# Layer norms as two fused VectorE operations a block, first norm without a trip through DRAM: one post-norm decoder layer on one core

## Chip, cores and metric

The kernel runs on one core of one Trainium2 chip. A core has TensorE (PE; its weight loads are listed as PEld), VectorE (DVE), ScalarE (ACT), GpSimd (POOL) and SyncE (SP, which here only issues transfers). The metric is the device time of one execution in microseconds (us), as a median over several runs.

## What is computed

One layer with 256 tokens of width 2048, all in float32. It has three sub-layers, and after each of them stands a layer norm over the residual sum:

```python
def layer_norm(x, g, b):
    mu = xf.mean(-1, keepdims=True)
    var = jnp.square(xf - mu).mean(-1, keepdims=True)
    return (xf - mu) * lax.rsqrt(var + LN_EPS) * g + b

y = hybrid_mixer(x, ...)              # two attention branches, gates, w_out
x = layer_norm(ALPHA * x + y, ln_g[0], ln_b[0])
y = mem_cross_attention(x, mem, ...)  # 4 heads into 256 memory tokens
x = layer_norm(ALPHA * x + y, ln_g[1], ln_b[1])
y = swiglu(x, w_ffn_in, w_ffn_out)    # width 5632
x = layer_norm(ALPHA * x + y, ln_g[2], ln_b[2])
```

## The kernel before, in words

**Products.** The 256 tokens are two tiles of 128 (`tt`). Every float32 operand is split into a rounded part and what the rounding leaves, and a product is three matmuls (L221 to L223). Weights stream from DRAM in chunks of 256 rows by 512 columns (`chunk_in`, L193): SP loads a chunk into `raw` (5 buffers), ScalarE writes the rounded half (L116), VectorE subtracts (L117), both into `hl` (4 buffers) or, for chunks that stay on chip, into a `b8` tile. A chunk serves 12 matmuls of 512 columns, 6 for each tile. Where `product` is called with `seq=8` (L242 to L253), the last eight chunks are used for the first tile alone, stay on chip, and then serve the second tile; there each third of four chunks (`i % 4 == 2`) has its subtraction done by GpSimd. Two products have `seq=8`: the first of the feed-forward (L827) and the last of the kernel (L848).

**Activations** are needed transposed, with their features on the partitions, as `Quad`s of 512 features by 256 tokens. `to_quad` (L153) makes half of one from a block of 128 tokens by 512 columns: four 128x128 transposes on TensorE (L156) into a PSUM tile `aux`, then a split (ScalarE L116, VectorE L117). `turn` (L168) makes a whole one from DRAM: four loads (L176), four 32x32-block transposes on VectorE (L181), a ScalarE copy (L182) and a VectorE subtraction (L184).

**Layer norms.** The class `Norm` (L664) adds a product to the residual on VectorE (L680) and takes its statistics (L681). `scales` (L683) aggregates them (L685), has GpSimd compute rstd with two tiny operations (L149, L150), and VectorE -mean * rstd (L689). `block` (L692) normalises 512 columns in place: ScalarE t * rstd - mean * rstd (L695), VectorE times g (L696), then plus b (L698), on GpSimd in the first norm and on even blocks of the second, on VectorE on its odd blocks. `run` (L700) does this block by block and makes the quads `lag` blocks later; blocks of columns named in `far` are written to DRAM (`keep`, L190) and come back through `turn`. `finish` (L722) is the last norm: ScalarE (L735), but VectorE for block 0 (L733), then VectorE times g (L739), GpSimd or VectorE plus b (L741), and the output (L742).

**Order.** The norms' steps are a generator in the queue `side`; `product` takes `steps` of it after each chunk, so that they are emitted between the chunks. The order in which the program emits is the priority from which a scheduler, at compile time, lays down each engine's fixed queue. The first norm (L772, both tiles, `lag` 6, quads 2 and 3 through DRAM) is emitted between chunks of the memory keys' product (`kc`, L774); its quads feed the query product `qc` (L779). The second norm (L811) runs tile by tile: the norm of tile 0 beside the `w_o_mem` products of tile 1, that of tile 1 beside the first tile's half of the first feed-forward product (L827). The last norm's `finish` is called as soon as a tile of the last product is done (L843).

Of the kernel before, what the change touches and what calls it, by code (L numbers as in the profile page):

```python
# [10 lines left out]
F32 = mybir.dt.float32  # L11
F32R = mybir.dt.float32r
AF = mybir.ActivationFunctionType
ALU = mybir.AluOpType
AX = mybir.AxisListType

P = 128
S = 256
NT = S // P
# [18 lines left out]
KC = 2  # L38
NTURN = 2
W = 512  # L40


class Side:
    """Work that is emitted in small steps between the chunks of the main products."""

# [20 lines left out]
def trunk(ctx: ExitStack, tc: tile.TileContext, a, out: bass.AP):  # L66
    nc = tc.nc
# [3 lines left out]
    work = ctx.enter_context(tc.tile_pool(name="work", bufs=2))  # L71
# [3 lines left out]
    side = Side()  # L75
    last = [None]
    later = []
# [9 lines left out]
    def nm(s):  # L87
        count[0] += 1
        return f"{s}_{count[0]}"
# [16 lines left out]
    class Quad:  # L106
        """Four blocks [128, 256] and what their rounding leaves, as operands of products."""

# [9 lines left out]

    # ---- constants
    ident = const.tile([P, P], F32, name="ident")  # L120
# [6 lines left out]
    for tt in range(NT):  # L127
        k = P * (tt + 1)
# [18 lines left out]
    def rstd(dst, var, scale):  # L147
        """(var * scale + eps) ** -0.5"""
        nc.gpsimd.tensor_scalar(dst, var, scale, EPS, op0=ALU.mult, op1=ALU.add)  # L149
        nc.gpsimd.tensor_tensor(dst, dst, mhalf, op=ALU.pow)  # L150

    # ---- transposes of [128 tokens, 512] into a quad
    def to_quad(q, tt, src):  # L153
# [10 lines left out]

    # ---- the same for 256 tokens, from DRAM: the loads put columns 128 a .. 128 a + 127 into partitions
    # 32 a .. 32 a + 31, so that transposes of 32 by 32 are all that is left. Partition p of block k holds
    # column 4 p + k (mixed), or column 32 k + p % 32 of those (not mixed).
    def turn(q, src, mixed=True):  # L168
# [22 lines left out]

    # ---- products with streamed weights: [256 tokens, kts * 128] @ [kts * 128, n]
    def chunk_in(pieces, c, n, held=False, mixed=False, fine=None, eng=None):  # L193
# [31 lines left out]
    def product(act, pieces, steps=1, before=None, first=None, seq=0, stream_seq=0, done=None):  # L225
        """act: quads; pieces: DRAM views of the weights' columns. The last seq chunks of weights stay on
        chip, and the first 128 tokens go through them before the others do."""
        n = sum(w.shape[1] for w in pieces)
        kts = pieces[0].shape[0] // P
        nchunk = kts // KC  # L230
        out = [ps_acc() for _ in range(NT)]
        for c in range(nchunk - seq):
            w = chunk_in(pieces, c, n, mixed=act[c * KC // 4].mixed, fine=first if c == 0 else None)
            if first is not None and c == 0:
                for _ in first:
                    pass
            if before is not None:
                before(c)
            for tt in range(NT):
                chunk_mm(out[tt], act, tt, c, kts, n, w)  # L240
            flush()
            side.step(steps)  # L242
        if seq:
            ws = []
            for i, c in enumerate(range(nchunk - seq, nchunk)):
                ws.append(chunk_in(pieces, c, n, held=i >= stream_seq, mixed=act[c * KC // 4].mixed, eng=nc.gpsimd if i % 4 == 2 else None))
                chunk_mm(out[0], act, 0, c, kts, n, ws[-1])
                side.step(steps)
            done(0, out[0])
            for i, c in enumerate(range(nchunk - seq, nchunk)):  # L250
                chunk_mm(out[1], act, 1, c, kts, n, ws[i])
                side.step(steps)
            done(1, out[1])  # L253
        elif done is not None:
            for tt in range(NT):
                done(tt, out[tt])
        return out
# [5 lines left out]

    # ---- inputs
    x, mem = a["x"][0], a["mem"][0]
# [19 lines left out]

    # ---- the weights of the latents
    ukT, uv = [], []
# [26 lines left out]

    # ---- indexer queries: [hi; lo] of a head on the partitions
    qi = []
# [18 lines left out]

    # ---- indexer keys, latents
    kvg = row_of(a["kv_norm_g"][0], LAT, "kvg")
# [9 lines left out]
    for tt in range(NT):  # L347
        sl = slice(tt * P, (tt + 1) * P)
        p = ps[tt]
# [31 lines left out]

    # ---- keys and values of the heads from the latents
    khT, vh = [], []
# [47 lines left out]

    # ---- attention of four heads
    def attention(q, kT, v, bias, slopes, oT, causal):
# [147 lines left out]

    # ---- gate of the first branch, before its sigmoid
    ma = [b8(F32) for _ in range(NT)]
# [5 lines left out]

    # ---- block attention: one block, so causal over all keys  # L590
    oTb = [None, None]
# [12 lines left out]
    for g in range(2):  # L604
# [4 lines left out]
        if g == 0:  # L609
            pass  # L610
    # the first branch must be done
    while oTa[1] is None or any(gen.__name__ == "dsa" for gen in side.queue):
# [34 lines left out]

    # ---- residual and layer norm
    tok = []
# [14 lines left out]
    class Norm:  # L664
        """Residual sums and the layer norm over them."""

# [15 lines left out]

        def scales(self, tt):  # L683
            mv = work.tile([P, 2], F32, tag="lnmv", name=nm("lnmv"))
            nc.vector.bn_aggr(mv, self.stats[tt])  # L685
            r = work.tile([P, 1], F32, tag="lnr", name=nm("lnr"))
            rstd(r, mv[:, 1:2], 1.0)
            m = work.tile([P, 1], F32, tag="lnm", name=nm("lnm"))
            nc.vector.tensor_scalar(m, mv[:, 0:1], r, -1.0, op0=ALU.mult, op1=ALU.mult)  # L689
            return r, m  # L690

        def block(self, tt, j, sc):  # L692
            cs = slice(j * W, (j + 1) * W)
            t = tok[tt][:, cs]
            nc.scalar.activation(t, t, AF.Identity, bias=sc[1], scale=sc[0])  # L695
            nc.vector.tensor_tensor(t, t, self.rows[0][:, cs], op=ALU.mult)  # L696
            eng = nc.vector if self.i > 0 and j % 2 else nc.gpsimd
            eng.tensor_tensor(t, t, self.rows[1][:, cs], op=ALU.add)  # L698

        def run(self, tts, lag, far=()):  # L700
            """Blocks of 512 columns: norm, then transposes some steps later; those in far through DRAM."""
            if self.quads is None:
                self.quads = [Quad() for _ in range(4)]
            sc = {tt: self.scales(tt) for tt in tts}
            todo = [(tt, j) for j in range(4) for tt in tts]
            spills = {j: spill() for j in far}
            for i in range(len(todo) + lag):
                if i < len(todo):
                    tt, j = todo[i]
                    self.block(tt, j, sc[tt])  # L710
                    if j in far:
                        keep(spills[j], tt, tok[tt][:, j * W:(j + 1) * W])
                if i >= lag:
                    tt, j = todo[i - lag]
                    if j not in far:
                        to_quad(self.quads[j], tt, tok[tt][:, j * W:(j + 1) * W])
                    elif tt == tts[-1]:
                        for _ in turn(self.quads[j], spills[j]):
                            yield
                yield  # L720

        def finish(self, tt):  # L722
            mv = work.tile([P, 2], F32, tag="lnmv", name=nm("lnmv"))
            nc.vector.bn_aggr(mv, self.stats[tt])
            r = work.tile([P, 1], F32, tag="lnr", name=nm("lnr"))
            rstd(r, mv[:, 1:2], 1.0)
            m = work.tile([P, 1], F32, tag="lnm", name=nm("lnm"))
            nc.vector.tensor_scalar(m, mv[:, 0:1], r, -1.0, op0=ALU.mult, op1=ALU.mult)
            for j in range(4):
                cs = slice(j * W, (j + 1) * W)  # L730
                t = tok[tt][:, cs]
                if j == 0:
                    nc.vector.tensor_scalar(t, t, mv[:, 0:1], r, op0=ALU.subtract, op1=ALU.mult)  # L733
                else:
                    nc.scalar.activation(t, t, AF.Identity, bias=m, scale=r)  # L735
            for j in range(4):
                cs = slice(j * W, (j + 1) * W)
                t = tok[tt][:, cs]
                nc.vector.tensor_tensor(t, t, self.rows[0][:, cs], op=ALU.mult)  # L739
                eng = nc.vector if j % 2 else nc.gpsimd  # L740
                eng.tensor_tensor(t, t, self.rows[1][:, cs], op=ALU.add)  # L741
                nc.sync.dma_start(out[0, tt * P:(tt + 1) * P, cs], t)  # L742

# [25 lines left out]

    # ---- cross-attention  # L770
    w_kv = a["w_kv_mem"][0]
    side.add(n1.run(range(NT), 6, (2, 3)))  # L772
    side.step(2)
# [40 lines left out]

    # ---- feed-forward
    hT = []
# [56 lines left out]
```

## Time and profile before

| what | us |
|---|---|
| median of 3 runs | 1504.6 |
| lowest and highest run | 1503.08, 1506.91 |
| profiled execution, first to last instruction | 1506.3 |

For the profiled execution no time is listed beside its span. Busy shares are of the span. In a timeline a row is: start, length, engine, line, operation, output<-inputs, shapes, how many instructions it merges, and in brackets how long the engine had been idle and what ended that. A matmul's length there contains its pipeline; the next one starts sooner. Groups by line give: how many, busy us, mean ns, and idle time before. `PEclk` is the share of TensorE's full clock that was granted.

### The profile page before, as it was taken

To read this page: it belongs to the slowest core of one execution; us is meant where nothing else is said; L and a number is where in the kernel's file an instruction comes from. 1 tells how busy PE (TensorE), PEld (TensorE's weight loads), DVE (VectorE), ACT (ScalarE), POOL (GpSimd) and SP (SyncE) were. 2 spreads that over 40 slices of the span, in tenths; PEclk is the share of its full clock that TensorE was granted. 3 is DMA by queue.
4 is the path that set the end of the run, shared out by engine and by line. 5 is a ranking of instruction groups with operands and counts; after the bars stand their busy time and mean duration, and the time that the engine had idled before them with its cause. 6 is when DMAs were issued, how large, how long until landed. Compare 5 with 4: busy or idle time off the path is not lost.

```text
span 1506.3 us, 17772 instructions
## 1 busy us (share of the span) xinstructions
PE 1464.6 (97%) x6640; PEld 1214.9 (81%) x6640; DVE 929.2 (62%) x1145; ACT 684.2 (45%) x798; POOL 55.6 (4%) x63
## 2 busy tenths in 40 slices
PE   7999999999999999889989999999999999999996
PEld 5988888888888887677878888888888888888885
DVE  6666986575756665776784555555455455545455
ACT  4645456454444443354753444444344444333342
POOL 0010000000000000040030000000000000000003
PEclk9999999999999999899999999999999999999998
DMA  9966667777667789749636667776777777666662
GB/s 272 235 181 185 193 207 233 220 251 224 206 200 224 230 257 281 192 141 298 204 117 201 208 210 222 222 220 204 231 217 204 223 219 248 193 200 190 194 218 88
DMA packets 201623, 318.71 MB, mean 212 GB/s; under 512 B 18880, under 2 KB 60992, under 8 KB 201536
## 3 DMA queue, kind: packets, MB, share of 16 engines
q1 hardware_dynamic: 201536, 317.57, 69.7%
q8 instruction: 52, 0.85, 0.2%
q14 instruction: 35, 0.29, 0.1%
HBM read 299.70 MB, written 17.83 MB: 211 GB/s over the span
## 4 chain that ended last, share of the span: by engine, by line
PE 51%; DVE 3%; DMA 1%; ACT 1%; issue 1%; POOL 0%; SPq 0%; ACTq 0%; DVEq 0%
PE acc L222 17%; PE acc L223 17%; PE acc L221 17%; DVE b L696 1%; DMA raw<-in_w_kv_mem 1%; DVE b L739 1%; PE aux L156 0%; ACT b L116 0%; DVE b L117 0%; DVE b L698 0%; DVE b L741 0%; DVE hl L117 0%; DVE lnst L681 0%; DVE b L680 0%; PE aux L261 0%
## 5 line engine op out<-in xcount | busy, mean ns | idle before, releaser
L117 DVE TENSOR_TENSOR hl<-raw,hl 128x1024 fp32r<-128x1024 f32 (+2 forms) x493 | 595.8, 1217 | 414.2 <-ACT hl L116 413.0
L116 ACT ACTIVATE hl<-raw 128x1024 fp32r<-128x1024 f32 (+2 forms) x495 | 516.2, 1051 | 592.4 <-PE acc L223 537.3
L222 PE MATMUL acc<-hl,b 128*128 128x512 f32 (+1 forms) x1976 | 771.8, 391 | 13.7 <-DVE hl L117 13.7
L221 PE MATMUL acc<-hl,b 128*128 128x512 f32 (+1 forms) x1976 | 769.5, 391 | 2.4 <-ACT b L182 1.7
L223 PE MATMUL acc<-hl,b 128*128 128x512 f32 (+1 forms) x1976 | 769.7, 390 | 1.1 <-DVE b L184 0.9
L222 PEld LDWEIGHTS acc<-hl,b 128*128 128x128 f32 x1976 | 373.3, 189 | 91.6 <-DVE hl L117 16.6
L221 PEld LDWEIGHTS acc<-hl,b 128*128 128x128 f32 x1976 | 373.3, 189 | 79.2 <-ACT b L182 2.5
L223 PEld LDWEIGHTS acc<-hl,b 128*128 128x128 f32 x1976 | 373.2, 189 | 78.8 <-DVE b L184 2.4
L181 DVE STREAM_TRANSPOSE tr<-turn 128x256 f32<-128x256 f32 (+1 forms) x156 | 71.3, 515 | 105.7 <-DMA turn<-spill 84.5
L182 ACT ACTIVATE b<-tr 128x1024 fp32r<-128x1024 f32 (+1 forms) x39 | 39.5, 1016 | 123.0 <-DVE tr L181 119.6
L184 DVE TENSOR_TENSOR b<-tr,b 128x1024 fp32r<-128x1024 f32 (+1 forms) x39 | 45.3, 1167 | 3.6 <-ACT b L182 3.0
L116 ACT ACTIVATE b<-aux 128x512 fp32r<-128x512 f32 (+1 forms) x44 | 23.2, 538 | 29.3 <-PE aux L262 15.5
L117 DVE TENSOR_TENSOR b<-aux,b 128x512 fp32r<-128x512 f32 (+1 forms) x44 | 26.1, 610 | 11.9 <-ACT b L116 11.7
L117 POOL TENSOR_TENSOR hl<-raw,hl 128x1024 fp32r<-128x1024 f32 x2 | 5.6, 2802 | 718.7 <-ACT hl L116 718.7
L222 PE MATMUL acc<-b,b 128*128 128x512 f32 x72 | 28.0, 391 | 0.3 <-DVE b L117 0.3
L221 PE MATMUL acc<-b,b 128*128 128x512 f32 x72 | 28.0, 393 | 0.1
L223 PE MATMUL acc<-b,b 128*128 128x512 f32 x72 | 27.9, 389 | 0.0
L117 DVE TENSOR_TENSOR b<-raw,b 128x1024 fp32r<-128x1024 f32 x16 | 23.1, 1461 | 7.7 <-ACT b L116 7.7
L261 PE MATMUL aux<-b,b 128*128 128x256 f32 (+1 forms) x80 | 21.9, 282 | 0.0
L116 ACT ACTIVATE b<-raw 128x1024 fp32r<-128x1024 f32 x18 | 18.4, 1059 | 5.9 <-DMA raw<-in_w_ffn_out 5.4
L262 PE MATMUL aux<-b,b 128*128 128x256 f32 (+1 forms) x80 | 21.0, 279 | 0.0
L260 PE MATMUL aux<-b,b 128*128 128x256 f32 (+1 forms) x80 | 20.8, 274 | 0.0
(129 smaller groups left out, 531.8 us busy)
## 6 DMA issues: line engine op xcount, KB each, us to landing
raw<-in_w_ffn_in SPq DMA_DIRECT2D x176, 512.0 KB, 4.5
raw<-in_w_in SPq DMA_DIRECT2D x143, 512.0 KB, 4.2
raw<-in_w_ffn_out SPq DMA_DIRECT2D x88, 512.0 KB, 4.2
raw<-in_w_out SPq DMA_DIRECT2D x32, 512.0 KB, 5.6
spill<-stage SPq DMA_DIRECT2D x56, 256.0 KB, 4.1
turn<-spill SPq DMA_DIRECT2D x112, 128.0 KB, 3.1
raw<-in_w_o_dsa SPq DMA_DIRECT2D x16, 512.0 KB, 4.5
raw<-in_w_o_moba SPq DMA_DIRECT2D x16, 512.0 KB, 4.2
```

The lines of the kernel that those rows point to most:

```text
L116: nc.scalar.activation(hi, src, AF.Copy)
L117: (eng or nc.vector).tensor_tensor(lo, src, f(hi), op=ALU.subtract)
L181: nc.vector.transpose(tr[:, i, :], v[:, i])
L182: nc.scalar.activation(hi, tr, AF.Copy)
L184: nc.vector.tensor_tensor(lo, tr, f(hi), op=ALU.subtract)
L221: nc.tensor.matmul(o[:, :n], xh, hi[:, kk, :n], start=k == 0, stop=False)
L222: nc.tensor.matmul(o[:, :n], xh, lo[:, kk, :n], start=False, stop=False)
L223: nc.tensor.matmul(o[:, :n], xl, hi[:, kk, :n], start=False, stop=k == kts - 1)
L260: nc.tensor.matmul(o, lh, rh, start=start, stop=False)
L261: nc.tensor.matmul(o, lh, rl, start=False, stop=False)
L262: nc.tensor.matmul(o, ll, rh, start=False, stop=stop)
L696: nc.vector.tensor_tensor(t, t, self.rows[0][:, cs], op=ALU.mult)
```

## The change

A block is now centred and scaled by two VectorE operations, `(t - mean) * g` and then `* rstd + b`. ScalarE and GpSimd no longer touch the blocks (GpSimd still computes rstd), and -mean * rstd is gone. The first norm runs with `lag` 4 and no `far` blocks: all its quads are made by `to_quad`. `finish` uses the same two operations, with the centring of two blocks ahead of the first scaling, and each block's output after its scaling. And the subtraction of each third of four held chunks goes from GpSimd to VectorE. Removed comments and docstrings are left out here.

```diff
@@ product, chunks with seq
-                ws.append(chunk_in(pieces, c, n, held=i >= stream_seq, mixed=act[c * KC // 4].mixed, eng=nc.gpsimd if i % 4 == 2 else None))
+                ws.append(chunk_in(pieces, c, n, held=i >= stream_seq, mixed=act[c * KC // 4].mixed))
@@ class Norm
         def scales(self, tt):
             mv = work.tile([P, 2], F32, tag="lnmv", name=nm("lnmv"))
             nc.vector.bn_aggr(mv, self.stats[tt])
             r = work.tile([P, 1], F32, tag="lnr", name=nm("lnr"))
             rstd(r, mv[:, 1:2], 1.0)
-            m = work.tile([P, 1], F32, tag="lnm", name=nm("lnm"))
-            nc.vector.tensor_scalar(m, mv[:, 0:1], r, -1.0, op0=ALU.mult, op1=ALU.mult)
-            return r, m
-
-        def block(self, tt, j, sc):
+            return mv[:, 0:1], r
+
+        def center(self, tt, j, sc):
             cs = slice(j * W, (j + 1) * W)
             t = tok[tt][:, cs]
-            nc.scalar.activation(t, t, AF.Identity, bias=sc[1], scale=sc[0])
-            nc.vector.tensor_tensor(t, t, self.rows[0][:, cs], op=ALU.mult)
-            eng = nc.vector if self.i > 0 and j % 2 else nc.gpsimd
-            eng.tensor_tensor(t, t, self.rows[1][:, cs], op=ALU.add)
+            nc.vector.scalar_tensor_tensor(t, t, sc[0], self.rows[0][:, cs], op0=ALU.subtract, op1=ALU.mult)
+
+        def scale(self, tt, j, sc):
+            cs = slice(j * W, (j + 1) * W)
+            t = tok[tt][:, cs]
+            nc.vector.scalar_tensor_tensor(t, t, sc[1], self.rows[1][:, cs], op0=ALU.mult, op1=ALU.add)
+
+        def block(self, tt, j, sc):
+            self.center(tt, j, sc)
+            self.scale(tt, j, sc)
...
         def finish(self, tt):
-            mv = work.tile([P, 2], F32, tag="lnmv", name=nm("lnmv"))
-            nc.vector.bn_aggr(mv, self.stats[tt])
-            r = work.tile([P, 1], F32, tag="lnr", name=nm("lnr"))
-            rstd(r, mv[:, 1:2], 1.0)
-            m = work.tile([P, 1], F32, tag="lnm", name=nm("lnm"))
-            nc.vector.tensor_scalar(m, mv[:, 0:1], r, -1.0, op0=ALU.mult, op1=ALU.mult)
+            sc = self.scales(tt)
+            for j in range(2):
+                self.center(tt, j, sc)
             for j in range(4):
+                self.scale(tt, j, sc)
+                if j + 2 < 4:
+                    self.center(tt, j + 2, sc)
                 cs = slice(j * W, (j + 1) * W)
-                t = tok[tt][:, cs]
-                if j == 0:
-                    nc.vector.tensor_scalar(t, t, mv[:, 0:1], r, op0=ALU.subtract, op1=ALU.mult)
-                else:
-                    nc.scalar.activation(t, t, AF.Identity, bias=m, scale=r)
-            for j in range(4):
-                cs = slice(j * W, (j + 1) * W)
-                t = tok[tt][:, cs]
-                nc.vector.tensor_tensor(t, t, self.rows[0][:, cs], op=ALU.mult)
-                eng = nc.vector if j % 2 else nc.gpsimd
-                eng.tensor_tensor(t, t, self.rows[1][:, cs], op=ALU.add)
-                nc.sync.dma_start(out[0, tt * P:(tt + 1) * P, cs], t)
+                nc.sync.dma_start(out[0, tt * P:(tt + 1) * P, cs], tok[tt][:, cs])
@@ cross-attention
-    side.add(n1.run(range(NT), 6, (2, 3)))
+    side.add(n1.run(range(NT), 4))
```

## Rows read from the trace of the kernel before

**Rows 1.** The page: each engine's busy us, share of the span and instructions.

```profile
PE 1464.6 (97%) x6640; PEld 1214.9 (81%) x6640; DVE 929.2 (62%) x1145; ACT 684.2 (45%) x798; POOL 55.6 (4%) x63
```

**Rows 2.** Busy time by stretch: us, PE, PEld, DVE, ACT, POOL, PEclk, DMA share, GB/s.

```profile
660.00:680.00 20.00, 15.82 (x65) 12.26 (x65) 19.70 (x15) 12.01 (x17) 14.08 (x8) 0.83 0.33 97
680.00:700.00 20.00, 20.00 (x88) 16.26 (x88) 13.89 (x18) 8.98 (x10) 0.00 (x0) 1.00 1.09 280
...
760.00:780.00 20.00, 17.12 (x76) 13.41 (x74) 19.58 (x23) 14.49 (x20) 8.77 (x7) 0.91 0.38 123
```

**Rows 3.** Timeline of VectorE, then of GpSimd, at the first norm.

```profile
656.70 0.38 DVE L685 BATCH_NORM_AGGREGATE lnmv<-lnst 128x2 f32<-128x24 f32 x2
657.48 1.23 DVE L117 TENSOR_TENSOR hl<-raw,hl 128x1024 fp32r<-128x1024 f32 x1 [0.40 <-ACT hl L116]
...
660.27 11.56 DVE L696 TENSOR_TENSOR b<-b,b 128x512 f32<-128x512 f32 x8 [0.36 <-ACT b L695]
671.75 5.63 DVE L117 TENSOR_TENSOR hl<-raw,hl 128x1024 fp32r<-128x1024 f32 x3
...
657.58 2.07 POOL L150 TENSOR_TENSOR lnr<-lnr,mhalf 128x1 f32<-128x1 f32 x2
661.09 14.08 POOL L698 TENSOR_TENSOR b<-b,b 128x512 f32<-128x512 f32 x8 [1.44 <-issue]
```

**Rows 4.** Timeline of TensorE behind the first norm: two waits.

```profile
674.09 0.80 PE L222 MATMUL acc<-hl,b 128*128 128x512 f32 x1 [3.77 <-DVE hl L117]
...
707.69 0.50 PE L222 MATMUL acc<-hl,b 128*128 128x512 f32 x1 [0.91 <-DVE hl L117]
```

**Rows 5.** Groups of instructions by line and shape, 640 to 800 us: GpSimd's additions.

```profile
L698 POOL TENSOR_TENSOR b<-b,b 128x512 f32<-128x512 f32 x12 | 20.3, 1717 | 7.3 <-DVE b L696 5.9 <-issue 1.4
```

**Rows 6.** The fused operation with a scalar per partition elsewhere: VectorE's groups, 130 to 180 us.

```profile
L561 DVE SCALAR_TENSOR_TENSOR score<-stage,widx,score 128x256 f32<-128x256 f32 x15 | 7.3, 483 | 0.6
L561 DVE SCALAR_TENSOR_TENSOR score<-stage,widx,score 128x128 f32<-128x128 f32 x15 | 5.2, 347 | 0.4
```

**Rows 7.** Timeline at the second norm: VectorE, ScalarE, then TensorE.

```profile
763.34 1.76 DVE L698 TENSOR_TENSOR b<-b,b 128x512 f32<-128x512 f32 x1
765.02 0.67 DVE L680 SCALAR_TENSOR_TENSOR b<-b,acc 128x512 f32<-128x512 f32 x1
765.62 0.68 DVE L698 TENSOR_TENSOR b<-b,b 128x512 f32<-128x512 f32 x1
...
773.43 3.18 DVE L117 TENSOR_TENSOR b<-raw,b 128x1024 fp32r<-128x1024 f32 x1 [0.17 <-ACT b L116]
...
768.56 4.84 ACT L116 ACTIVATE b<-raw 128x1024 fp32r<-128x1024 f32 x5
...
761.71 0.66 PE L156 MATMUL aux<-ident,b 128*128 128x128 f32 x4
...
768.16 0.39 PE L221 MATMUL acc<-hl,b 128*128 128x512 f32 x1
...
779.01 0.66 PE L156 MATMUL aux<-ident,b 128*128 128x128 f32 x4 [0.47 <-POOL b L698]
...
785.29 0.40 PE L223 MATMUL acc<-hl,b 128*128 128x512 f32 x1
```

**Rows 8.** Timeline of the end: first tile's sum, second tile's last matmul and norm.

```profile
1484.48 0.69 DVE L680 SCALAR_TENSOR_TENSOR b<-b,acc 128x512 f32<-128x512 f32 x1 [6.84 <-PE acc L223]
...
1491.98 0.39 PE L223 MATMUL acc<-b,b 128*128 128x512 f32 x1
...
1493.78 0.68 DVE L680 SCALAR_TENSOR_TENSOR b<-b,acc 128x512 f32<-128x512 f32 x1
...
1495.22 0.26 DVE L724 BATCH_NORM_AGGREGATE lnmv<-lnst 128x2 f32<-128x24 f32 x1
...
1495.85 0.55 POOL L150 TENSOR_TENSOR lnr<-lnr,mhalf 128x1 f32<-128x1 f32 x1
...
1502.40 0.69 DVE L741 TENSOR_TENSOR b<-b,b 128x512 f32<-128x512 f32 x1
```

## The prediction

> **What bounds the kernel now.** I read the page first: TensorE is busy 1464.6 us of a span of 1506.3 [rows 1]. Only its 41.7 us of idle time and what it runs at a lowered clock can be won, whatever VectorE (62%) or ScalarE (45%) save. The stretches show where: most are like 680 to 700, full and at full clock, 88 matmuls in 20 us, so 0.227 us each and 2.72 us for a chunk's twelve; 660 to 680 and 760 to 780 have TensorE at 15.82 and 17.12 us and clock 0.83 and 0.91, with VectorE full (19.70, 19.58) [rows 2]. These are the first and second norm. The third place is the end, where after the last matmul nothing but the last norm is left [rows 8].
>
> Then the timelines. **First norm:** VectorE takes 11.56 us for eight multiplications by g, and only then the three weight splits, for the first of which TensorE waits 3.77 us, until 674.09 [rows 3, 4]. GpSimd's additions run beside this, eight in 14.08 us. The reader is to see that the two engines slow each other: in the second norm a VectorE addition took 1.76 us beside GpSimd and 0.68 right afterwards, and a split 3.18 us against 1.23 [rows 7, 3]. **Second norm:** from 761.71 to 768.16 and from 779.01 to 785.29 TensorE does transposes and a few matmuls in fits [rows 7]. These are 12.7 us; 28 transposes at 0.66 us for four would be 4.6 us even at that pace, and eight matmuls 1.8, so some 6 to 7 us are lost. **End:** the last matmul is over at 1492.4, but the residual sum starts at 1493.78, because VectorE is still in the first tile's norm; the last write of the norm ends at 1503.09 [rows 8].
>
> A measurement of this kernel can tell about 0.3%, 4.5 us, from no change.
>
> **Price of the new operation.** The fused operation with two SBUF tensors and a scalar per partition took 483 ns for 256 columns and 347 for 128 [rows 6], so 136 ns per 128 columns and 483 + 2 x 136 = 755 ns for 512. The next independent one starts about 0.07 us before the end of the one in front (765.02 + 0.67 against 765.62 [rows 7]): one each 0.69 us. Where a scaling follows its own centring I count the whole 0.755. A block is then 1.445 us, and eight are 11.6 us: just what the eight multiplications take now beside GpSimd [rows 3]. VectorE gains nothing in length; what it gains is that ScalarE's and GpSimd's steps (1.7 us an addition [rows 5]) no longer stand before and behind it.
>
> **The end.** The aggregation starts at 1495.22 and ends at 1495.48. A centring needs only the mean, so two can run while GpSimd makes rstd: to 1496.94. Six operations are left from 1496.88: 5 x 0.69 + 0.755 = 4.2, to 1501.1 against 1503.09, 2.0 us less. But GpSimd may not get at its operands meanwhile. In the first norm its two power operations took 2.07 us next to VectorE's L117, while one alone took 0.55 [rows 3, 8]: 1.0 us more. That L117 also reads two SBUF tensors, as a centring does; no row shows the fused form beside GpSimd. If the first centring goes in front of rstd and the second in between, rstd ends 1.45 us later than its 1496.40, the first scaling starts at 1497.85, the last ends at 1502.05: 1.0 us less. I take this end, since the two-tensor L117 is the nearest row. The first tile's norm also ends earlier by as much, and the residual sum starts 1.0 us earlier (at most 1.4, when TensorE is done). Sum 2.0 us, at most 3.4.
>
> The Trainium skill, "SBUF — State Buffer", section "Who interferes with whom", says that a VectorE instruction with two SBUF inputs and a GpSimd instruction that reads SBUF exclude each other for a whole instruction. It names no exception for the fused form, so by it the end gains 2.0 us; with no such exclusion it would gain 3.4. The pair of power operations agrees with it for the plain two-tensor form.
>
> **The first norm.** The first centring can start at 657.1, as the aggregations end; the first multiplication now starts at 660.27 [rows 3]. With 11.6 us and up to 1.7 us for rstd, the sixteen end between 668.8 and 670.5, against 671.83. The split behind them takes 1.2 us instead of a third of 5.63, so that TensorE could go on at 670.0 to 671.7 instead of 674.09: 2.4 to 4.1 us. Against this stand the quads that now go through TensorE: four more `to_quad`, 16 transposes (at most 2.6 us, inside the wait if one is left), and four more splits. All eight such splits are emitted ahead of the later weight chunks and each costs VectorE about 0.6 us, as a plain operation of this size (0.68 less 0.07 [rows 7]): if all go first, that is 4.8 us more and TensorE goes on at 674.8 to 676.5, up to 2.4 us later. If one more weight chunk slips behind them, a further 1.6 us or so are lost. From -4 to +4 us; nothing decides the queue's order, and I take the middle, 0.
>
> **The trip through DRAM.** It takes away four writes, eight loads on SP's queue, eight VectorE transposes and two splits. While these run, TensorE is full (20.00 of 20 us [rows 2]), so the trip itself is hidden; its place in the queue may have made the one wait at 707.69, 0.91 us [rows 4]. I take 0.4 of 0 to 0.9.
>
> **The second norm.** VectorE gets more to do: 16 fused operations (8 blocks x 1.445 = 11.6) for 12 plain ones (12 x 0.6 = 7.2), and two weight splits of 1.2 that GpSimd had, one before the norm; it loses four tiny operations and what GpSimd's additions and splits added to it: 1.1 on an addition and 2.0 on a split in the rows shown [rows 7], with two or three more such places. So 6.8 more against 5 to 6 less: about even. What changes is the path: rstd, then ScalarE, VectorE, GpSimd is now rstd, then one VectorE operation; and the second tile's norm no longer queues on ScalarE behind five weight conversions of 4.84 us together [rows 7]. I count 2.4 of the 7 us lost there as won: between nothing, if VectorE's length decides, and 6. If weight splits slip behind the norm here as well, 4 us are lost instead.
>
> **GpSimd's split in the last product** costs nothing: VectorE waits 6.84 us for TensorE before the first tile's sum [rows 8], and 2 x 1.2 us fit. Without that cover it would be 2.4 us.
>
> **Sum:** 2.0 + 0 + 0.4 + 2.4 = 4.8 us. The profiled execution's 1506.3 (1.7 over the median) becomes 1501.5, the median 1504.6 becomes **1499.8**.
>
> **Rivals.** *VectorE's length decides (25%).* Both norms stay as long as they are, since one VectorE operation replaces work that three engines shared; only the end is won. For it: VectorE is full in both stretches [rows 2] and 11.6 equals 11.56. Against it: the 3 us of later start. 1504.6 - 2.0 = 1502.6, no change that can be told.
>
> *The norms stop holding TensorE (18%).* The splits fall between the fused operations, so TensorE hardly waits: 3.4 at the end, 3 in the first norm, 0.9, and 5 in the second: 12 us, 1492. For it: every mutual slowdown goes. Against: the count of VectorE's work just made.
>
> *Weight splits queue behind the norm (12%), slower.* The place is VectorE's queue in both norms. Four `hl` buffers hold 48 matmuls, 10.9 us at 0.227 (half as long where a chunk serves only one tile): it decides when the norm work put in one piece in front of a split is longer than that. Sixteen fused operations and eight splits would be 11.6 + 4.8 = 16.4 us. Price: 4 us in the first norm, 4 in the second, 2 more at the lowered clock around a long wait (a granted clock of 0.83 over 20 us [rows 2] is 3.4 us of work at full clock, part of it inside the wait), less 2.0 at the end: 8 us, 1512.6.
>
> *The change does less than it says (5%):* the trip through DRAM was hidden and nothing else moves: that ends as the first rival does.
>
> **Numbers.** The forecast has 40%, with a range of its own of 1497.5 to 1502.5 (0 to 0.9 for the trip, two us either way in a norm). Three fifths of it lie below 1500.1, the bound of faster: 0.24; with the second rival 0.18, and 0.05 from the first and the last, if the end gains all of 3.4 and a norm a little: 0.47. Slower 0.12, and one hundredth for an order that I have not thought of: 0.13. The rest, 0.40, is no change. The range runs from the second rival's 1492 to 1508, which takes in a slower rival at half its price and leaves out about one in ten on either side.
>
> **What would show it.** Right: the residual sum of the second tile at 1492.8 or earlier by this clock, the last write some 1.0 us sooner after it; fused operations of about 0.755 us, never over 1; GpSimd with only tiny operations; wait before the first norm's weight split between 2 and 5 us; less than 6 us lost in the second. Wrong: fused operations that differ much from 0.755 us, a wait of TensorE for a weight split of over 6 us in either norm, more than one stretch at a lowered clock in each, or any change in the feed-forward between the second norm and the end.

## The result, and the profile after

| | before | after |
|---|---|---|
| median, us (4 runs each) | 1505.76 | 1489.49 |
| lowest and highest, us | 1503.08, 1506.97 | 1485.75, 1490.49 |
| profiled execution's span, us | 1506.3 | 1483.6 |

The changed kernel takes 0.9892 of the time before, with a 95% interval of 0.9876 to 0.9908: 16.3 us faster, where 4.8 were forecast. The measured time lies outside the range given.

The page of the changed kernel, its line of engines, answers to [rows 1]:

```profile
PE 1455.7 (98%) x6656; PEld 1209.4 (82%) x6656; DVE 919.0 (62%) x1151; ACT 669.6 (45%) x778; POOL 21.1 (1%) x43
```

TensorE is busy 8.9 us less although it has 16 transposes more, and its idle time falls from 41.7 to 27.9 us. GpSimd drops from 55.6 to 21.1.

**Where the time went.** The two profiles can't be compared from their start: at the last pair of residual sums ahead of the first norm (VectorE, L680) they already differ by 7.6 us (653.19 against 645.55), although the instructions up to there stand in the same order in both kernels. That scatter belongs to no part of the change (the same changed kernel, run again as e8_after below, comes to this point at 650.39), so the stages are counted from those sums on. The boundaries are instructions that both kernels have: the second copy of the memory keys' product (ScalarE L425), the first residual sum of the `w_o_mem` product (L680), the end of the last matmul, the end of the span. The first three in the kernel before, then in the changed one:

```profile
653.19 1.28 DVE L680 SCALAR_TENSOR_TENSOR b<-b,acc 128x512 f32<-128x512 f32 x2
684.58 0.60 ACT L425 ACTIVATE stage<-acc 128x512 f32<-128x512 f32 x1 [0.76 <-PE acc L223]
749.72 1.28 DVE L680 SCALAR_TENSOR_TENSOR b<-b,acc 128x512 f32<-128x512 f32 x2
...
645.55 1.28 DVE L680 SCALAR_TENSOR_TENSOR b<-b,acc 128x512 f32<-128x512 f32 x2
670.02 0.60 ACT L425 ACTIVATE stage<-acc 128x512 f32<-128x512 f32 x1 [0.54 <-PE acc L223]
734.24 1.28 DVE L680 SCALAR_TENSOR_TENSOR b<-b,acc 128x512 f32<-128x512 f32 x2
```

| stage, us | before | after | less by |
|---|---|---|---|
| first norm, to the copy of the memory keys | 31.39 | 24.47 | 6.9 |
| from there to the second norm (holds the trip through DRAM) | 65.14 | 64.22 | 0.9 |
| second norm and feed-forward, to the last matmul | 742.65 | 739.24 | 3.4 |
| end, behind the last matmul | 13.93 | 10.12 | 3.8 |
| sum | 853.11 | 838.05 | 15.1 |

The 15.1 us of the table and the 16.3 of the medians differ by less than single executions of one kernel do. A stage is read from one execution too: in kernels that leave it as it was, the second row varies by 1.2 us and the third by 2 (table in the experiments).

**First norm.** The busy time by stretch of the changed kernel (columns as in [rows 2]); by this clock the first norm's work lies in the first two rows, the second norm's in the last two:

```profile
640.00:660.00 20.00, 20.00 (x90) 16.52 (x89) 17.01 (x25) 7.80 (x8) 2.31 (x4) 1.00 0.46 141
660.00:680.00 20.00, 20.00 (x106) 17.01 (x105) 16.50 (x20) 11.56 (x17) 0.00 (x0) 1.00 0.78 254
740.00:760.00 20.00, 16.38 (x76) 12.37 (x74) 20.00 (x32) 8.40 (x11) 3.20 (x4) 1.00 0.25 82
760.00:780.00 20.00, 19.85 (x95) 16.49 (x96) 12.32 (x15) 7.46 (x11) 0.00 (x0) 1.00 0.57 186
```

TensorE never stops in the first norm, at full clock. Before, it was idle there for 4.2 of 20 us and its granted clock was 0.83 on the mean [rows 2]: behind the wait of 3.77 us [rows 4] its matmuls came 0.43 us apart until 679.5, the lower of its two levels (1.2 GHz), and 0.23 apart from there. 0.17 of the 15.82 busy us are 2.7 more. Together that is 6.9 us, what the table gives. The second norm still costs TensorE 3.6 us, in this execution in one stretch. Of the third row's 3.4 us, 2.8 come up to the second Silu copy of the feed-forward (ScalarE; 48.05 us behind the first `w_o_mem` sum before, 45.22 now), so in the norm itself; the other 0.6 lie farther on, within the scatter.

The timeline of the changed kernel at the first norm, VectorE, then GpSimd, then TensorE, answers to [rows 3, 4]:

```profile
649.07 0.38 DVE L686 BATCH_NORM_AGGREGATE lnmv<-lnst 128x2 f32<-128x24 f32 x2
649.37 5.41 DVE L694 SCALAR_TENSOR_TENSOR b<-b,lnmv,b 128x512 f32<-128x512 f32 x8
654.70 1.21 DVE L117 TENSOR_TENSOR hl<-raw,hl 128x1024 fp32r<-128x1024 f32 x1
655.84 2.73 DVE L699 SCALAR_TENSOR_TENSOR b<-b,lnr,b 128x512 f32<-128x512 f32 x4
658.49 1.21 DVE L117 TENSOR_TENSOR hl<-raw,hl 128x1024 fp32r<-128x1024 f32 x1
659.62 2.07 DVE L699 SCALAR_TENSOR_TENSOR b<-b,lnr,b 128x512 f32<-128x512 f32 x3
661.61 1.21 DVE L117 TENSOR_TENSOR hl<-raw,hl 128x1024 fp32r<-128x1024 f32 x1
...
650.27 1.61 POOL L150 TENSOR_TENSOR lnr<-lnr,mhalf 128x1 f32<-128x1 f32 x2
...
659.90 1.91 PE L156 MATMUL aux<-ident,b 128*128 128x128 f32 x16
```

The reader is to see three things. The first centring starts 0.3 us behind the start of the aggregations; before, the first multiplication started 3.6 us behind it. Weight splits stand between the fused operations, each 1.21 us long, and the longest piece of norm work ahead of one is 5.41 us; before, 11.56 us of multiplications stood in one piece, and three splits behind them took 5.63. And the first 16 transposes (four calls of `to_quad`) take 1.91 us without a wait.

The waits of TensorE over the whole changed kernel (us in total, times, longest):

```profile
PE acc L222 <- DVE hl L117: 6.8, 6, 2.0
...
PE aux L156 <- DVE b L699: 1.4, 1, 1.4
```

The first line in the kernel before:

```profile
PE acc L222 <- DVE hl L117: 13.7, 6, 3.8
```

Between 630 and 800 us, where both norms lie, the changed kernel has no wait of this kind left.

**The end** of the changed kernel, timeline of TensorE, VectorE and GpSimd, answers to [rows 8]:

```profile
1473.09 0.39 PE L223 MATMUL acc<-b,b 128*128 128x512 f32 x1
...
1473.52 0.69 DVE L680 SCALAR_TENSOR_TENSOR b<-b,acc 128x512 f32<-128x512 f32 x1 [1.70 <-PE acc L223]
...
1474.97 0.26 DVE L686 BATCH_NORM_AGGREGATE lnmv<-lnst 128x2 f32<-128x24 f32 x1
1475.26 2.74 DVE L694 SCALAR_TENSOR_TENSOR b<-b,lnmv,b 128x512 f32<-128x512 f32 x4
1477.92 2.73 DVE L699 SCALAR_TENSOR_TENSOR b<-b,lnr,b 128x512 f32<-128x512 f32 x4
...
1475.32 0.75 POOL L149 TENSOR_SCALAR lnr<-lnmv 128x1 f32<-128x1 f32 x1 [7.07 <-DVE lnmv L686]
1476.15 0.94 POOL L150 TENSOR_TENSOR lnr<-lnr,mhalf 128x1 f32<-128x1 f32 x1
```

The residual sum starts 0.04 us after the last matmul (1.41 before), since VectorE is through with the first tile. All four centrings come before the first scaling; rstd is ready at 1477.09, held up, but 0.8 us before the scalings begin. From the sum to the last write it is 7.13 us instead of 9.31.

### The profile page after: what moved, and what is told of

Same layout as the page of the kernel before. It is cut to its first block, busy times and chain, and to the rows that moved or that the text cites. A ratio compares the mean times of both kernels' runs of the same rounds, so it can differ in the third digit from the quotient of the medians.

```text
span 1483.6 us, 17739 instructions
## 1 busy us (share of the span) xinstructions
PE 1455.7 (98%) x6656; PEld 1209.4 (82%) x6656; DVE 919.0 (62%) x1151; ACT 669.6 (45%) x778; POOL 21.1 (1%) x43
## 4 chain that ended last, share of the span: by engine, by line
PE 92%; DVE 3%; DMA 3%; issue 1%; SPq 1%; ACT 0%; DVEq 0%
PE acc L223 29%; PE acc L222 29%; PE acc L221 29%; DMA turn<-in_mem 2%; DMA turn<-in_x 1%; PE aux L261 1%; PE aux L262 1%; PE aux L260 1%; DVE hl L117 1%; DVE tr L181 1%; DVE b L680 0%; DVE b L694 0%; PE aux L156 0%; SPq L176 0%; DVE lnst L681 0%
## 5 line engine op out<-in xcount | busy, mean ns | idle before, releaser
L181 DVE STREAM_TRANSPOSE tr<-turn 128x256 f32<-128x256 f32 (+1 forms) x148 | 66.9, 510 | 96.6 <-DMA turn<-spill 80.7
L223 PE MATMUL acc<-b,b 128*128 128x512 f32 x72 | 27.9, 389 | 0.0
L817 ACT ACTIVATE stage<-acc 128x512 f32<-128x512 f32 x22 | 13.2, 599 | 19.6 <-PE acc L223 19.6
L261 PE MATMUL aux<-b,b 128*128 128x256 f32 (+1 forms) x80 | 21.8, 281 | 0.0
L680 DVE SCALAR_TENSOR_TENSOR b<-b,acc 128x512 f32<-128x512 f32 x24 | 15.7, 680 | 9.7 <-PE acc L223 9.7
L262 PE MATMUL aux<-b,b 128*128 128x256 f32 (+1 forms) x80 | 21.0, 279 | 0.0
L116 ACT ACTIVATE b<-raw 128x1024 fp32r<-128x1024 f32 x18 | 18.4, 1058 | 5.7 <-DMA raw<-in_w_ffn_out 5.3
```

Source lines behind the costliest of these rows:

```text
L116: nc.scalar.activation(hi, src, AF.Copy)
L181: nc.vector.transpose(tr[:, i, :], v[:, i])
L223: nc.tensor.matmul(o[:, :n], xl, hi[:, kk, :n], start=False, stop=k == kts - 1)
L261: nc.tensor.matmul(o, lh, rl, start=False, stop=False)
L262: nc.tensor.matmul(o, ll, rh, start=False, stop=stop)
L680: nc.vector.scalar_tensor_tensor(tok[tt][:, cs], tok[tt][:, cs], ALPHA, p, op0=ALU.mult, op1=ALU.add)
```

## Experiments

Two theories were set against each other. **Contention** (D in the expectations): GpSimd's additions hold up VectorE's operations with two SBUF inputs, and taking GpSimd off the blocks is what pays. **Path and order** (E): the blocks' shorter way and the place of the weight splits between the norm's operations pay, whatever GpSimd does. Each kernel was timed against the kernel before on the same chip.

| kernel | median, us | before, us | ratio, 95% interval |
|---|---|---|---|
| e1_block | 1492.28 | 1504.65 | 0.9915 [0.9897, 0.9933] |
| e2_finish | 1502.51 | 1504.65 | 0.9987 [0.9969, 1.0004] |
| e3_nofar | 1504.01 | 1504.65 | 0.9993 [0.9977, 1.0008] |
| e4_split | 1503.17 | 1504.65 | 0.9998 [0.9983, 1.0014] |
| e5_vadd | 1493.72 | 1505.70 | 0.9926 [0.9909, 0.9944] |
| e6_beside | 1499.34 | 1505.70 | 0.9956 [0.9942, 0.9971] |
| e7_behind | 1496.98 | 1505.70 | 0.9947 [0.9932, 0.9961] |
| e8_after (the changed kernel) | 1489.24 | 1505.70 | 0.9895 [0.9878, 0.9912] |

One of the twelve executions of e4_split took 8426.66 us; why isn't known, and the figures above leave it out.

Their stages, cut as above (us):

| kernel | first norm | to second norm | to last matmul | end |
|---|---|---|---|---|
| e1_block | 24.46 | 64.26 | 739.05 | 13.87 |
| e2_finish | 30.57 | 66.32 | 742.30 | 11.53 |
| e3_nofar | 32.12 | 64.08 | 740.71 | 13.65 |
| e4_split | 30.55 | 66.29 | 743.34 | 13.15 |
| e5_vadd | 25.06 | 65.01 | 738.81 | 13.87 |
| e6_beside | 28.17 | 67.92 | 742.46 | 10.16 |
| e7_behind | 31.47 | 63.22 | 739.90 | 10.07 |
| e8_after | 24.46 | 64.43 | 739.21 | 10.11 |

### The change in four parts: e1 to e4

**e1_block**: the kernel before, with only the blocks of the first two norms fused.

```diff
...
-            nc.scalar.activation(t, t, AF.Identity, bias=sc[1], scale=sc[0])
-            nc.vector.tensor_tensor(t, t, self.rows[0][:, cs], op=ALU.mult)
-            eng = nc.vector if self.i > 0 and j % 2 else nc.gpsimd
-            eng.tensor_tensor(t, t, self.rows[1][:, cs], op=ALU.add)
...
+            self.center(tt, j, sc)
+            self.scale(tt, j, sc)
```

Not shown: `scales` without -mean * rstd, and the new `center` and `scale`, all as in the change.

> The kernel before with only the blocks of the first two norms fused (centre and scale on VectorE); the trip through DRAM, GpSimd's weight splits and the old end stay. Theory A (the gain of the norms comes from the blocks themselves: no GpSimd beside VectorE, and weight splits standing between the fused operations in VectorE's queue): 9 to 12 us faster than before, of which 6 to 7 in the first norm (from the residual sums of w_out's last columns to the second copy of the memory keys about 24.5 to 25.5 us instead of 31.4), no wait of TensorE for a weight split over 1 us there, and 2 to 4 in the second. Theory B (it comes from the quads that no longer go through DRAM): at most 3 us faster, the first norm still at 28 us or more.

Measured: 12.4 us less, a little over the upper end. The first norm and the stage to the last matmul are those of the changed kernel. In 630 to 800 us no wait of TensorE for a streamed weight split is left; the largest in e1's list of waits is for splits into tiles that stay on chip (quads and held chunks):

```profile
PE acc L222 <- DVE b L117: 2.2, 3, 1.4
```

So all of the gain ahead of the end that the profiles show is in these lines, with the trip through DRAM and GpSimd's splits still in place.

**e2_finish**: only the last norm fused.

```diff
...
-                if j == 0:
-                    nc.vector.tensor_scalar(t, t, mv[:, 0:1], r, op0=ALU.subtract, op1=ALU.mult)
-                else:
-                    nc.scalar.activation(t, t, AF.Identity, bias=m, scale=r)
...
+            for j in range(2):
+                self.center(tt, j, sc)
+            for j in range(4):
+                self.scale(tt, j, sc)
+                if j + 2 < 4:
+                    self.center(tt, j + 2, sc)
...
```

> The kernel before with only the last norm fused. From the first tile's last residual sum to the end of the span 18.9 us instead of 21.8, so 2.9 us faster, and nothing else moves. If the end's gain came from somewhere else (GpSimd's weight splits in the last product), less than 1 us.

Measured: 2.1 us less by the medians, an interval that takes in no change, and 2.4 in the profile's last stage (19.4 us from the first tile's last sum, where 18.9 were expected). The changed kernel's profiles show 3.8 there. From the sum to the last write e2 takes the same 7.13 us; what it lacks lies behind the last write, 4.36 us to the end of the span against 2.95. Why the last transfers took longer in that one execution wasn't tried.

**e3_nofar**: only the trip through DRAM removed.

```diff
-    side.add(n1.run(range(NT), 6, (2, 3)))
+    side.add(n1.run(range(NT), 4))
```

> The kernel before with only the first norm's quads all made by transposes on TensorE (lag 4, nothing through DRAM). Theory A: within 1.5 us of before, TensorE's wait for the weight split still 3 to 5 us, since VectorE's queue still has eight multiplications beside GpSimd's additions in front of it. Theory B: 5 to 8 us faster.

Measured: nothing that can be told. The first norm gets 0.7 us longer, the next stage 1.1 shorter: 32 transposes instead of 16 now fall into the first. TensorE's wait for the weight split stays at 3.8 us, as theory A had it.

**e4_split**: only GpSimd's weight splits moved to VectorE.

```diff
-                ws.append(chunk_in(pieces, c, n, held=i >= stream_seq, mixed=act[c * KC // 4].mixed, eng=nc.gpsimd if i % 4 == 2 else None))
+                ws.append(chunk_in(pieces, c, n, held=i >= stream_seq, mixed=act[c * KC // 4].mixed))
```

> The kernel before with only GpSimd's weight splits moved to VectorE. Theory A: within 1.5 us of before, either way. Theory C (GpSimd's splits were what slowed VectorE in the second norm): 2 to 4 us faster, all of it between the first sum of w_o_mem and the second Silu copy (48.0 us before).

Measured: nothing that can be told. The four parts alone are worth 12.4, 2.1, 0.6 and 1.5 us. That they add up to 16.6, about as much as the change, is in part chance: only the first by itself is more than the measurement leaves open.

### What in the blocks pays: e5 to e8

**e5_vadd** sets contention against path and order. ScalarE's step, the multiplication, the addition, the trip and everything else stay; only the engine of the additions changes. The path gets shorter only by what an addition takes less on VectorE (0.68 us) than on GpSimd (1.72 [rows 5]).

```diff
-            eng = nc.vector if self.i > 0 and j % 2 else nc.gpsimd
-            eng.tensor_tensor(t, t, self.rows[1][:, cs], op=ALU.add)
+            nc.vector.tensor_tensor(t, t, self.rows[1][:, cs], op=ALU.add)
```

> The kernel before with one word changed: the additions of b in the first two norms all on VectorE, as plain two-tensor operations; ScalarE's first step stays, and in VectorE's queue of the first norm twelve norm operations still stand in front of the next weight split. Theory D (GpSimd's additions beside VectorE made the norms slow, by holding up VectorE's operations with two SBUF tensors): no multiplication over 0.75 us, the first norm at 25 to 28 us instead of 31.4, 4 to 9 us faster in all. Theory E (the place of the weight splits in VectorE's queue and the shorter path made the difference): at most 2 us faster, TensorE's wait for a weight split still 3 us or more.

Measured: 12.0 us less, more than the upper end, and as much as the fused blocks of e1. Nothing was fused and no operation was taken away; VectorE got twelve more. VectorE's groups by line and shape, 640 to 800 us (how many, busy us, mean ns, idle before), first of the kernel before, where L698 in the same view has 4 additions in 4.9 us:

```profile
L696 DVE TENSOR_TENSOR b<-b,b 128x512 f32<-128x512 f32 x16 | 18.4, 1197 | 0.4 <-ACT b L695 0.4
```

then of e5_vadd:

```profile
L697 DVE TENSOR_TENSOR b<-b,b 128x512 f32<-128x512 f32 x16 | 10.6, 682 | 0.0
L696 DVE TENSOR_TENSOR b<-b,b 128x512 f32<-128x512 f32 x16 | 10.5, 683 | 0.4 <-ACT b L695 0.4
```

and of the changed kernel:

```profile
L699 DVE SCALAR_TENSOR_TENSOR b<-b,lnr,b 128x512 f32<-128x512 f32 x16 | 11.2, 747 | 0.0
L694 DVE SCALAR_TENSOR_TENSOR b<-b,lnmv,b 128x512 f32<-128x512 f32 x16 | 10.9, 745 | 0.0
```

Twenty operations took VectorE 23.3 us (18.4 + 4.9); thirty-two take 21.1 once GpSimd is out of the way, and the fused ones 22.1. E, which gave this edit little or nothing, falls as the whole cause: fourteen norm operations still stand in one piece ahead of the next weight split, 8.6 us long now, and TensorE doesn't wait for that split. VectorE's timeline of e5_vadd there:

```profile
653.14 1.23 DVE L117 TENSOR_TENSOR hl<-raw,hl 128x1024 fp32r<-128x1024 f32 x1 [0.40 <-ACT hl L116]
...
655.93 1.40 DVE L696 TENSOR_TENSOR b<-b,b 128x512 f32<-128x512 f32 x2 [0.36 <-ACT b L695]
...
664.47 2.35 DVE L117 TENSOR_TENSOR hl<-raw,hl 128x1024 fp32r<-128x1024 f32 x2
```

**e6_beside** puts the contention back into the changed kernel. The additions into `junk` are extra work that no one reads; GpSimd does them, as often as it did before.

```diff
         def block(self, tt, j, sc):
             self.center(tt, j, sc)
             self.scale(tt, j, sc)
+            if self.i == 0 or j % 2 == 0:
+                cs = slice(j * W, (j + 1) * W)
+                junk = work.tile([P, W], F32, tag="junk", name=nm("junk"), bufs=1)
+                nc.gpsimd.tensor_tensor(junk, tok[tt][:, cs], self.rows[1][:, cs], op=ALU.add)
```

> The changed kernel with GpSimd additions put back beside the fused operations where the kernel before had them (all blocks of the first norm, the even ones of the second), but into a scratch tile that nobody reads: extra work, VectorE's queue in the same order, no step in any path. Theory D: fused operations and weight splits beside it stretched to 1.2 us and more (splits to 2), TensorE waits for a split again, the first norm at 28 to 32 us instead of 24.5, the second 1 to 3 us longer, 5 to 10 us slower than the changed kernel (1494 to 1500). Theory E: within 1.5 us of the changed kernel.

Measured: 10.1 us more than e8_after, which ran beside it, just over the 5 to 10 that D had. The same view of e6_beside:

```profile
L699 DVE SCALAR_TENSOR_TENSOR b<-b,lnr,b 128x512 f32<-128x512 f32 x16 | 19.3, 1249 | 0.0
L694 DVE SCALAR_TENSOR_TENSOR b<-b,lnmv,b 128x512 f32<-128x512 f32 x16 | 10.8, 741 | 0.0
```

and its timeline at the first norm, VectorE, GpSimd, TensorE:

```profile
663.72 5.26 DVE L699 SCALAR_TENSOR_TENSOR b<-b,lnr,b 128x512 f32<-128x512 f32 x3
668.91 2.32 DVE L117 TENSOR_TENSOR hl<-raw,hl 128x1024 fp32r<-128x1024 f32 x1
...
672.87 4.58 DVE L117 TENSOR_TENSOR hl<-raw,hl 128x1024 fp32r<-128x1024 f32 x2
...
660.77 17.86 POOL L707 TENSOR_TENSOR junk<-b,b 128x512 f32<-128x512 f32 x8 [4.12 <-DVE b L699]
...
671.29 0.50 PE L222 MATMUL acc<-hl,b 128*128 128x512 f32 x1 [2.16 <-DVE hl L117]
```

The centrings ran before GpSimd's additions began and keep their 741 ns; the scalings take 1249 on the mean (747 in the changed kernel), single ones up to 1814, a split 2.32 us for 1.21, and TensorE waits for it again. No other engine waits for the additions: they cost by their place beside VectorE alone. The three stages up to the last matmul lose 3.7, 3.5 and 3.2 us against e8. Of the 3.2, 2.5 come up to the second Silu copy (47.70 against 45.19 us), nearly all that the change won there. The 3.5 in the middle, where no addition of e6 runs, are a wait of 1.8 us for one weight split and a granted clock of 0.91 from 700 to 720 us; why they come there wasn't tried.

**e7_behind** tests the order. In the changed kernel the weight splits that come up behind the first norm are held until all sixteen fused operations are issued.

```diff
+            if behind[0] is None:
+                split(hi[:, k, :n], lo[:, k, :n], raw[:, k, :n], eng)
+            else:
+                with tc.issue_after(behind[0].ins):
+                    split(hi[:, k, :n], lo[:, k, :n], raw[:, k, :n], eng)
...
-            nc.vector.scalar_tensor_tensor(t, t, sc[1], self.rows[1][:, cs], op0=ALU.mult, op1=ALU.add)
+            behind[0] = nc.vector.scalar_tensor_tensor(t, t, sc[1], self.rows[1][:, cs], op0=ALU.mult, op1=ALU.add)
+            if self.i or (tt, j) != (NT - 1, 3):
+                behind[0] = None
...
```

> The changed kernel with the weight splits of the memory keys' later chunks held in VectorE's queue behind all sixteen fused operations of the first norm (the slower rival of the prediction, made by an order alone; the work is the same). The first waiting split ends about 661.5 by the changed kernel's clock, when TensorE has had chunks for 8 us and transposes for 2: a wait of 4 to 6 us and some 2 us of lowered clock, the first norm at 30 to 34 us instead of 24.5, so 5 to 9 us slower than the changed kernel (1494 to 1499). If the order does not matter (theory D alone), within 1.5 us of it.

Measured: 7.7 us more than e8_after. By the profiles the first norm is 7.0 us longer; 1.9 of these are sixteen transposes that the changed kernel makes in the next stage, so some 5 are lost. TensorE's wait for the split is 2.25 us, less than the 4 to 6 expected; it also waits for scalings, 1.29 us in the row below. Its timeline there, VectorE, then TensorE (five lines were added above, so L704 is the scaling, L118 the split, L157 the transposes, L227 the second matmul):

```profile
652.33 5.40 DVE L699 SCALAR_TENSOR_TENSOR b<-b,lnmv,b 128x512 f32<-128x512 f32 x8
657.64 5.38 DVE L704 SCALAR_TENSOR_TENSOR b<-b,lnr,b 128x512 f32<-128x512 f32 x8
662.95 4.62 DVE L118 TENSOR_TENSOR hl<-raw,hl 128x1024 fp32r<-128x1024 f32 x4
...
660.43 1.53 PE L157 MATMUL aux<-ident,b 128*128 128x128 f32 x12 [1.29 <-DVE b L704]
...
664.22 0.50 PE L227 MATMUL acc<-hl,b 128*128 128x512 f32 x1 [2.25 <-DVE hl L118]
```

and its busy time by stretch:

```profile
660.00:680.00 20.00, 17.31 (x82) 14.38 (x83) 16.55 (x21) 8.13 (x12) 0.00 (x0) 0.91 0.62 209
```

VectorE works at full pace, and still TensorE waits and its granted clock goes down to 0.91 in the stretch, because 10.7 us of norm work stand in one piece ahead of the split. So D, by which the order should not matter, falls as the whole cause too: the order is a second condition. The length of the piece goes with it: from the end of one weight split to the end of the next it was 14.4 us here and 15.3 in the kernel before, and TensorE waited; it was 11.3 in e5, and TensorE did not. Where between these the wait begins wasn't tried, and in e6, where one delay followed another, 7.4 us were enough. The next stage, without those transposes, gives 1.2 us back. In the first norm, undoing the order loses some 5 of the 6.9 us gained and putting GpSimd back about half of them (3.7 us).

**e8_after**: the changed kernel once more, as the measure for e6 and e7.

> The changed kernel again, beside the others on the same chip: ratio to before 0.988 to 0.991; the first norm 24.5 us, the second 45, the end 18.9 as in its first profile.

Measured: 0.9895, as the first time, with the same stages.

## Why the prediction was wrong in its size

The sign and the price of the new operation were right. The case that came was the second rival, "the norms stop holding TensorE" (18%, 12 us), and even that was short: it had 3 us for the first norm, where 6.9 came, and 5 for the second, where 2.8 to 3.4 did, so that its total came as near as it did partly by luck.

**Price of the new operation: right.** 755 ns were worked out, 745 and 747 measured, one each 0.68 (eight in 5.41 us); none is over 0.78 us.

**The end: wrong, 2.0 for 3.8.** The step was "I take this end": rstd is held up by the centrings, so the first scaling comes later. It was held up: L149 took 0.75 us and L150 0.94, against 0.19 and 0.57 in the first tile's part of the second norm, where VectorE was at statistics as they began. But the scheduler put all four centrings ahead of the scalings, and VectorE had work for longer than GpSimd needed. The other end of that estimate, 3.4 (1.4 for the earlier sum and 2.0 behind it), is what came: 1.37 and 2.18, with 0.25 behind the last write. The Trainium skill, "SBUF — State Buffer", section "Who interferes with whom", has a VectorE instruction with two SBUF inputs and a GpSimd one that reads SBUF exclude each other. The rows agree as far as they go, for the fused form too: in e6, with GpSimd's additions beside it, the scaling took 1249 ns on the mean instead of 747. What was drawn from it, a later end, did not follow, since a delay costs only where someone waits.

**The first norm: wrong, 0 for 6.9, and the largest part.** The step was "nothing decides the queue's order, and I take the middle, 0", within -4 to +4. The start 3 us earlier and the splits at 1.2 us came as counted. Two things did not. The feared queue of eight quad splits in front of the weight splits didn't form: the splits that stream weights fell between the fused operations. And the term had only TensorE's wait in it. The lowered clock of that stretch, of which the first paragraph said that "what it runs at a lowered clock can be won", was put into the slower rival but not into this sum; it is 2.7 us by [rows 2], and the interval of the term would have had to reach to about 7. What decided was both the order and the disturbance: holding the splits back costs some 5 of the 6.9 us (e7), GpSimd's additions beside the scalings 3.7 (e6).

**The trip through DRAM: not told apart from nothing.** 0.4 of 0 to 0.9 was taken. The stage gives 0.9, but not by the trip: e1, which keeps it, has 64.26 us there, against 64.22 and 64.43 in the changed kernel, and e3, which only drops it, shows nothing in all that can be told.

**The second norm: near in size, 2.4 for 2.8** (3.4 counted to the last matmul) within 0 to 6, **but not by its reason.** "About even" for VectorE's length was nearly right: its stretch is full (20.00 of 20 us) and TensorE still loses 3.6 us there. The prediction put the gain down to the path: rstd, one operation, transposes. But e5 gets as much here with ScalarE's step still in the path (45.25 us to the second Silu copy), and e6 loses 2.5 us with the new path and GpSimd beside it. So the shorter path needs no credit; GpSimd out of VectorE's way is enough, and that the number came out is in part luck.

**GpSimd's split in the last product: right**, nothing: VectorE waits 1.70 us for TensorE in the changed kernel even before the last sum.

**What the sum missed.** The mutual slowdown was seen ("the two engines slow each other"), yet it was priced only at the places shown in the rows, 1.1 us here and 2.0 there, and the eight multiplications of 11.56 us were taken as a length to be equalled. At 0.6 us each they need 4.8; the other 6.8 were GpSimd's (in e5, with ScalarE's step still ahead of them, none took over 0.69). Had that been counted, a version without any fusing would have stood beside the change as a rival, and that is e5: three quarters of the gain from one line.

## What to carry to other kernels

Where an engine that feeds TensorE runs longer than its own undisturbed rows, price the disturbance first: count its instructions at the undisturbed duration, and call the rest what it is. Taking the disturbing engine out, even by giving its work to the disturbed one, may pay as much as the fusing one had in mind (here 12.0 us against 12.4). And keep long pieces of side work divisible: the time between two weight splits in VectorE's queue decided beside its total load.

## What the runs showed of the hardware

- GpSimd's addition of 128x512 beside VectorE's fused operation makes both slow: VectorE's scaling 1249 ns on the mean for 747, GpSimd's addition some 2.2 us (eight in 17.86), where the shortest of them took 1.29. The other way round, GpSimd's two operations of 128x1 for rstd were stretched where VectorE was at splits and centrings. The timeline of GpSimd in the changed kernel, second norm, first and second tile:

```profile
743.48 0.19 POOL L149 TENSOR_SCALAR lnr<-lnmv 128x1 f32<-128x1 f32 x1 [35.98 <-DVE lnmv L686]
743.75 0.57 POOL L150 TENSOR_TENSOR lnr<-lnr,mhalf 128x1 f32<-128x1 f32 x1
754.19 1.04 POOL L149 TENSOR_SCALAR lnr<-lnmv 128x1 f32<-128x1 f32 x1 [9.87 <-DVE lnmv L686]
755.31 1.41 POOL L150 TENSOR_TENSOR lnr<-lnr,mhalf 128x1 f32<-128x1 f32 x1
```

  So 0.76 us became 2.45; VectorE's four centrings took 2.7 us in both places.
- Fusing bought VectorE no time: a fused operation took 745 ns where a plain one took 682, and 32 fused ones 22.1 us where 32 plain ones took 21.1. What it saved was ScalarE's step, and GpSimd's.
- Transposes of 128x128 in float32 went by at 0.12 us each (16 in 1.91) when nothing was waited for; the prediction had them at 0.16.
